# Issue orders in a first stage, and one FFN block wholly in seven-product form

## The chip, the cores and the metric
The kernel runs on one core of a Trainium2 chip. The metric is the device time of one execution in microseconds (us); the median of the runs is compared. Engines: TensorE (PE in the profile, PEld its weight loads), VectorE (DVE), ScalarE (ACT), GpSimd (POOL), and SyncE (SP), whose queue issues the DMAs.

## What is computed
Two pre-norm residual layers on a sequence of 1024 with width 1024, all float32. Layer 0 mixes with a Mamba-2 SSD mixer, layer 1 with a causal Conformer convolution, each is followed by a dense SwiGLU FFN of width 2816, and a final RMSNorm ends it:

```python
for i in range(DEPTH):
    if i % 2 == 0:
        h = h + mamba2_mixer(rmsnorm(h, ssm_norm), w_in, conv_w, ..., w_out)
    else:
        h = h + conformer_conv_module(rmsnorm(h, cv_norm), w_pw1, ..., w_pw2)
    h = h + swiglu_ffn(rmsnorm(h, ffn_norm[i]), ffn_w_gate[i], ffn_w_up[i], ffn_w_down[i])
return rmsnorm(h, final_norm)
```

`mamba2_mixer` projects `u` to 5152 columns (gate, the inputs of a causal convolution of four taps, and 32 columns for `dt`), convolves, runs the state-space scan in chunks of 128, norms with the gate and projects back.

## The kernel before, in words
Activations stand transposed: 128 partitions hold 128 of the 1024 features, the free dimension holds tokens. The sequence is cut into two blocks of 512 tokens (0 and 1), so that one tile is 128x512 and a block of `h` is eight of them. Every matrix product is done three times, on high and low halves of both operands: `split` (L233) makes a high half by a copy on ScalarE and a low half by a subtraction on VectorE (or GpSimd). `gemm` (L255) multiplies low by high, high by low, high by high. Weights come by DMA into `wst` (two buffers), are split into `whi`, `wlo` (four each), and used.

The program is written as a list of units that `run` (L1196) puts together and `emit` (L1285) traces in order; loads are traced ahead of the units that use them. A scheduler then makes each engine's queue: among the instructions that it takes for ready, the one traced first goes first, loads and weight preparation having a head start of 60 places. Queues run strictly in that order on the chip.

**The first stage.** `consts` (L147) makes constants. `begin` (L551) fetches block 0 of `x` and the first three weight tiles of the in-projection, splits them, adds up the squares of `x` and returns the unit `products` (L607), which multiplies three weight tiles and the `dt` columns with the raw `x` times the norm's gain, as the factor that the norm gives each token can be applied to the product. `norm_u` (L324) takes the square sums (`rstd_a`, `rstd_b` with its matmuls at L310), makes the factor, keeps it in `fac`, and writes the normed input `u` in halves, the low ones partly on GpSimd. `in_proj` (L515) makes ten tiles per group of heads: tiles 0 to 3 are made from raw `x` (tile 3 as the unit `r3`), 4 to 9 from `u`. Tiles 0 to 5 go through `conv4` (L492): into a buffer `raws` (by VectorE with `fac`, L503, or by ScalarE, L501), then the four taps; tiles 6 to 9 are the gate. `dt_pre` (L417) transposes the `dt` columns on TensorE (L428) and computes their softplus, `dt_post` (L452) makes decays with small matmuls (L462, L463, L478). `selects` (L185) and `halves` (L209) make small constants. `ssd` (L628) is the scan: `prep`, `A(z)`, `B(z)` (L680, L681), `decay`, `C(z)`. Eight PSUM banks are dealt out by `banks`; a bank is written again only when its reader is done.

**The last FFN.** `ffn` (L925) has two forms. The regular form multiplies each 128 columns of gate and up with `u` in 24 matmuls of 128x512. The fast form, `seven` (L832), treats two column tiles at a time as 2x2 blocks of features and token halves and needs seven block products in place of eight: seven units `p1`, `p2`, `p6`, `p7`, `p5`, `p3`, `p4` of twelve matmuls of 128x256 (L881). For that VectorE sums blocks of the weights (L850 to L852), and `sums_u` (L783) makes sums of blocks of `u` once (tiles `ru`, `tu`). The partial results move out of two shared banks by ScalarE (L892, L901, L908) and VectorE (L897, L909, L917). `chain7` (L1009) orders products of successive tiles and puts down projections (`dn`, L977) between them as soon as their hidden tiles are there. `final` (L1169) norms and sends out a block; its scalings are at L1189.

In the last layer block 0 ends with eight down projections of six tiles. Then block 1 runs two column tiles in the regular form, and twenty in the fast form (groups of 6, 6, 4 and 4). `sums_u(1)` stands between the regular units, `final(0)` after the second and third unit.

Of the kernel before, what the change touches and what calls it, by code (L numbers as in the profile page):

```python
# [43 lines left out]
WARM = 13  # L44
HALO = 30
# [63 lines left out]
class Trunk:  # L109
# [75 lines left out]
    def selects(self):  # L185


        nc = self.nc
        tt = nc.vector.tensor_tensor
        t = self.small.new("sels")  # L190
        rows, one = (t[:, 16 * i:16 * i + 16].rearrange("p (k h) -> p k h", k=2) for i in range(2))
        idg = lambda g: self.ident[:, 32 * g:32 * g + 16].rearrange("p (k h) -> p k h", k=2)
        tt(rows, idg(0), idg(1), ALU.add)
        tt(rows, rows, idg(2), ALU.add)
        tt(rows, rows, idg(3), ALU.add)
        tt(one[:, 0], rows[:, 0], rows[:, 1], ALU.add)
# [9 lines left out]
        nc.vector.tensor_copy(self.sel, one[:, 0].unsqueeze(2).to_broadcast([P, 8, 64]))  # L206
        self.small.drop(t)
# [95 lines left out]
    def rstd_b(self, x, n, tag="ss", w=T):  # L303
# [5 lines left out]
        for k, y in enumerate(x if whole else x[::-1]):  # L309
            nc.tensor.matmul(bc, self.ones if whole else self.onesr, y[:, :w], start=k == 0, stop=k == len(x) - 1)  # L310
# [181 lines left out]
    def conv4(self, b, c, acc, dst, fac=None):  # L492
        nc = self.nc
        raw = self.raws[self.nraw % 2]
        self.nraw += 1
# [19 lines left out]
    def in_proj(self, i, u=None, fac=None):  # L515
# [12 lines left out]
        def run(n):  # L528
# [3 lines left out]
            if n < 2:  # L532
                self.conv4(b, 16 + 4 * n + g, acc, self.c_bc[:, 2 * n + par], fac)
            elif n < 6:
                if n == 2:
                    self.XS[i] = self.big.new("xs")
                self.conv4(b, 4 * g + n - 2, acc, self.XS[i][:, n - 2], fac if n < NR else None)
            else:
                if n == 6:
                    self.SZ[i] = self.big.new("sz")  # L540
                s = self.SZ[i][:, n - 6]
                self.nc.scalar.activation(s, acc, AF.Tanh, scale=0.5)
                self.nc.vector.scalar_tensor_tensor(s, s, 1.0, acc, op0=ALU.add, op1=ALU.mult)
        units = [Unit(lambda n=n: run(n), lambda n=n: load(n)) for n in range(10)]
        if u is not None:
            self.W_in = W
            return [Unit(lambda n=n: gemm(n), lambda n=n: load(n)) for n in range(NB, NR)], [
# [3 lines left out]
    def begin(self, raw, load_dt):  # L551
# [19 lines left out]
        def split_x(d):  # L571
# [3 lines left out]
            nc.vector.scalar_tensor_tensor(lo, x[d], g, hi.bitcast(F32), op0=ALU.mult, op1=ALU.subtract)  # L575
# [9 lines left out]
        fetch_x(0)  # L585
        load_dt()
# [9 lines left out]
        for d in range(KD):  # L596
            split_x(d)
# [28 lines left out]
        return Unit(products), bigs  # L626
# [569 lines left out]
    def run(self):  # L1196
# [6 lines left out]
        self.consts()  # L1203
        self.mixer_setup()
# [3 lines left out]
        r3, ip = self.in_proj(0, raw, fac)  # L1208
# [3 lines left out]
        r3[0].load()  # L1212
        r3[0].load = None
        nu = self.norm_u(0, "ssm_norm", 0, fac, (0, 1, 3, 5, 7))
        q = [products] + nu[:2] + [call(self.halves, fac)] + nu[2:] + r3 + [call(lambda: self.big.drop(*rb))]
        q += dt[1:2] + [call(self.selects)] + dt[2:] + ip[:NR]
        q += [call(lambda: self.small.drop(fac)), call(lambda: self.banks(mm=(0, 1, 2, 3), ss=(4, 5, 6, 7)))] + ip[NR:]
        q += [call(self.load_x, 1)]
        for i in range(8):
# [16 lines left out]
            q += weave(self.ssd(i), fill) + post  # L1236
# [141 lines left out]
```

## Time and profile before

| | us |
|---|---|
| median of 3 runs (lowest, highest) | 2493.28 (2493.01, 2493.83) |
| the profiled execution | 2493.91 |
| its span, first to last instruction | 2492.2 |
| TensorE busy in the span | 2471.1 |
| VectorE busy | 2052.9 |
| ScalarE busy | 1328.7 |
| mean granted TensorE clock | 0.997 |

The profile is of one execution. Times in it are counted from the start of the span. An instruction's row gives start and duration, or the duration of several that follow each other; matmuls are pipelined, so their spacing and not their duration tells what they cost. What a row names as the releaser is what the engine's idle time ended with.

### The profile page before, as it was taken

The page shows a single profiled execution, that of the slowest core. Times are in us where ns is not written, and L with a number is a line of the kernel's source. Part 1 is how long each engine was busy: PE and PEld are TensorE (multiplying, and loading weights), DVE is VectorE, ACT ScalarE, POOL GpSimd, SP SyncE. Part 2 cuts the span into 40 slices and gives each one's busy share as a digit, 9 for nine tenths or more (in the row PEclk, how much of TensorE's full clock was granted, in tenths as well). Part 3 has the DMA queues.
Part 4 walks back from the last instruction along what each step waited for, and adds up shares of the span by engine and source line. Part 5 has one row for each costly group of instructions (what it writes and reads, how often), then busy time and mean ns, then how long its engine had stood idle before and what let it go on. Part 6 is the DMA issues. An engine that isn't in the chain of part 4 may idle for free.

```text
span 2492.2 us, 35811 instructions
## 1 busy us (share of the span) xinstructions
PE 2471.1 (99%) x13752; PEld 2114.9 (85%) x13752; DVE 2052.9 (82%) x3030; ACT 1328.7 (53%) x2365; POOL 398.8 (16%) x406
## 2 busy tenths in 40 slices
PE   8999999999999999999999999999999999999998
PEld 6788887888887899998888789988887899899998
DVE  7988989878889886768799797778997977986675
ACT  5776776766667553545333455453335545554444
POOL 1212111112111000000444410004444100000000
PEclk9999999999999999999999999999999999999999
DMA  4222222222223332323223233232232323332322
GB/s 159 68 68 85 77 62 85 77 73 79 76 70 110 89 112 92 110 67 100 93 93 111 87 114 109 64 102 93 93 119 85 123 91 104 131 118 82 119 85 73
DMA packets 69516, 233.54 MB, mean 94 GB/s; under 512 B 7648, under 2 KB 11232, under 8 KB 61920
## 3 DMA queue, kind: packets, MB, share of 16 engines
q1 hardware_dynamic: 69344, 231.25, 28.5%
q8 instruction: 108, 1.77, 0.3%
q14 instruction: 64, 0.52, 0.1%
HBM read 227.02 MB, written 4.19 MB: 93 GB/s over the span
## 4 chain that ended last, share of the span: by engine, by line
PE 97%; DVE 2%; ACT 1%; issue 0%; DMA 0%; DVEq 0%; SPq 0%; ACTq 0%
PE p L259 68%; PE p L881 23%; PE p L712 1%; PE p L704 1%; PE p L667 1%; PE p L680 1%; PE p L681 1%; PE p L310 0%; PE p L647 0%; PE p L695 0%; DVE wlo L235 0%; PE p L408 0%; PE p L614 0%; PE p L615 0%; PE p L618 0%; DVE un_s L349 0%
## 5 line engine op out<-in xcount | busy, mean ns | idle before, releaser
L234 ACT ACTIVATE whi<-wst 128x512 fp32r<-128x512 f32 (+1 forms) x652 | 388.0, 597 | 689.3 <-PE p L259 577.9
L259 PE MATMUL p<-uhi_b,wlo 128*128 128x512 f32 x1344 | 533.7, 397 | 3.3 <-ACT uhi_b L234 1.8
L259 PE MATMUL p<-ulo_b,whi 128*128 128x512 f32 x1344 | 529.4, 394 | 1.6 <-POOL ulo_b L235 1.1
L259 PE MATMUL p<-uhi_b,whi 128*128 128x512 f32 x1344 | 530.5, 395 | 0.0
L259 PE MATMUL p<-hid_b,whi 128*128 128x512 f32 x1344 | 419.1, 394 | 0.2
L235 DVE TENSOR_TENSOR wlo<-wst,whi 128x512 fp32r<-128x512 f32 (+1 forms) x442 | 303.9, 690 | 123.5 <-ACT whi L234 120.2
L235 POOL TENSOR_TENSOR wlo<-wst,whi 128x512 fp32r<-128x512 f32 x208 | 256.4, 1236 | 724.3 <-ACT whi L234 720.9
L881 PE MATMUL p<-uhi_b,wh_b 128*128 128x256 f32 x1856 | 343.9, 280 | 0.0
L259 PEld LDWEIGHTS p<-uhi_b,wlo 128*128 128x128 f32 x1344 | 253.0, 188 | 62.4 <-ACT uhi_b L234 2.6
L259 PEld LDWEIGHTS p<-ulo_b,whi 128*128 128x128 f32 x1344 | 253.3, 188 | 61.9 <-POOL ulo_b L235 2.9
L259 PEld LDWEIGHTS p<-uhi_b,whi 128*128 128x128 f32 x1344 | 253.1, 188 | 59.2 <-issue 0.3
L259 PEld LDWEIGHTS p<-hid_b,whi 128*128 128x128 f32 x1344 | 251.9, 188 | 56.7 <-DVE hid_b L235 1.1
L881 PEld LDWEIGHTS p<-uhi_b,wh_b 128*128 128x128 f32 x1856 | 290.9, 188 | 3.2 <-ACT vw_s L908 0.8
L259 PE MATMUL p<-hid_b,wlo 128*128 128x512 f32 x672 | 264.3, 394 | 0.0
L881 PE MATMUL p<-ulo_b,wh_b 128*128 128x256 f32 x928 | 259.9, 280 | 0.0
L881 PE MATMUL p<-tu_b,wh_b 128*128 128x256 f32 x1392 | 183.2, 281 | 0.0
L881 PEld LDWEIGHTS p<-ulo_b,wh_b 128*128 128x128 f32 x928 | 174.6, 188 | 2.0
L234 ACT ACTIVATE wh_b<-ws_b 128x1024 fp32r<-128x1024 f32 x116 | 122.7, 1059 | 99.2 <-PE p L881 38.9
L881 PEld LDWEIGHTS p<-tu_b,wh_b 128*128 128x128 f32 x1392 | 173.6, 188 | 1.3
L1097 DVE SCALAR_TENSOR_TENSOR p<-ci_b,par,p 128x507 f32<-128x507 f32 (+29 forms) x240 | 160.3, 733 | 3.3 <-ACT p L1094 2.0
L235 DVE TENSOR_TENSOR wh_b<-ws_b,wh_b 128x1024 fp32r<-128x1024 f32 x116 | 141.1, 1221 | 25.6 <-ACT wh_b L234 25.3
L1099 DVE SCALAR_TENSOR_TENSOR p<-ci_b,par,p 128x512 f32<-128x512 f32 x232 | 158.1, 749 | 1.9 <-ACT p L1094 1.4
(282 smaller groups left out, 4027.1 us busy)
## 6 DMA issues: line engine op xcount, KB each, us to landing
wq_b<-w_gu SPq DMA_DIRECT2D x58, 1024.0 KB, 4.8
wst<-w_in SPq DMA_DIRECT2D x77, 512.0 KB, 3.5
wst<-w_dn SPq DMA_DIRECT2D x88, 384.0 KB, 3.1
wst<-w_gu SPq DMA_DIRECT2D x60, 512.0 KB, 3.5
wst<-w_pw SPq DMA_DIRECT2D x48, 512.0 KB, 3.5
wst<-w_out SPq DMA_DIRECT2D x64, 256.0 KB, 2.6
wst<-w_dn SPq DMA_DIRECT2D x40, 256.0 KB, 2.7
h<-xT SPq DMA_DIRECT2D x8, 512.0 KB, 8.8
```

Source lines behind the costliest of these rows:

```text
L234: self.nc.scalar.activation(hi, src, AF.Copy)
L235: (eng or self.nc.vector).tensor_tensor(lo, src, hi.bitcast(F32), ALU.subtract)
L259: self.nc.tensor.matmul(acc, a, b, start=n == 0, stop=n == tot - 1)
L667: nc.tensor.transpose(xt[:, zs(j)], self.XS[i][:, j, zs(z)], self.ident)
L680: nc.tensor.matmul(sg, self.gtr, aml, start=True, stop=False)
L681: nc.tensor.matmul(sg, self.gtr, amh, start=False, stop=True)
L704: nc.tensor.matmul(O[:, zs(j)], H[:, zs(j)], CT[:, zs(z)], start=True, stop=True)
L712: nc.tensor.matmul(Y[po:po + 64, zs(hh // 2)], self.XDT[z % 2][:, hh * 64:(hh + 1) * 64], E[:, zs(r)], start=True, stop=True)
L881: nc.tensor.matmul(to, x, y, start=n == 0 and not more, stop=n == 11, skip_group_check=True)
L1097: nc.vector.scalar_tensor_tensor(acc[:, s:], x[:, HALO:TW - s], w(s), acc[:, s:], op0=ALU.mult, op1=ALU.add)
L1099: nc.vector.scalar_tensor_tensor(acc if s < 30 else c, x[:, HALO - s:TW - s], w(s), acc, op0=ALU.mult, op1=ALU.add)
```

## The change
In the first stage: `selects` moves to the front and keeps program order on VectorE, and `begin`'s instructions on VectorE go behind it. The squares of `x` keep program order on ScalarE in pairs. `products` is cut in two: tiles 0 to 5 of the features before the norm's matmuls, tiles 6 and 7 and then `r3` behind them. `halves` goes behind the last low half of `x` on VectorE. `conv4` is cut into `conv4a` (into the buffer) and `conv4b` (the taps); the unit `evict` does `conv4a` for tiles 0 to 3 at once, into the two `raws` and two spare stretches of `ms`. `dt_post` goes on TensorE behind the last matmul of tile 7, with the priority of the place ahead of tile 0's unit; the first three units of `ssd(0)` go on TensorE behind the last matmul of tile 9. Seven banks are dealt to `mm` and one to `ss` until tile 5. `issue_after(ins)` orders only instructions of the engine of `ins`, and only their issue.

In the last FFN: all 22 column tiles of block 1 take the fast form (groups of 6, 6, 6 and 4); `sums_u(1)` and the norm of block 1 move in between the last down projections of block 0.

```diff
+NP = 6
     def selects(self):
-        nc = self.nc
-        tt = nc.vector.tensor_tensor
+        nc, keep = self.nc, self.tc.keep_in_program_order
+        tt = lambda *a: keep(nc.vector.tensor_tensor(*a))
...
-    def conv4(self, b, c, acc, dst, fac=None):
-        nc = self.nc
-        raw = self.raws[self.nraw % 2]
-        self.nraw += 1
+        self.conv4b(b, c, self.conv4a(b, c, acc, fac), dst)
+
+    def conv4a(self, b, c, acc, fac=None, raw=None):
+        nc = self.nc
+        if raw is None:
+            raw = self.raws[self.nraw % 2]
+            self.nraw += 1
...
+        def evict():
+            ms = self.c_ms.rearrange("p a t -> p (a t)")
+            spare = [ms[:, 1014 + 516 * k:1014 + 516 * k + T + 3] for k in range(2)]
+            for n, raw in enumerate(self.raws + spare):
+                W["raw", n] = True
+                W["acc", n] = self.conv4a(b, 16 + 4 * n + g if n < 2 else 4 * g + n - 2, W["acc", n], fac, raw)
...
+        def square(d):
+            to = s if d == 0 else self.small.new("sq")
+            self.tc.keep_in_program_order(nc.scalar.activation(to, x[d], AF.Square))
+            if d:
+                nc.vector.tensor_tensor(s, s, to, ALU.add)
+                self.small.drop(to)
...
-            if d > 1:
-                self.sq_add(("h", 0), x[d - 2])
-        for d in range(KD - 2, KD):
-            self.sq_add(("h", 0), x[d])
+            if d % 2:
+                square(d - 1)
+                square(d)
...
+        def rest(r3):
+            with self.tc.issue_after(self.norm_mm.ins):
+                products(NP, KD)
+                r3()
+        return lambda r3: [Unit(lambda: products(0, NP)), Unit(lambda: rest(r3))], bigs
...
         self.consts()
+        self.selects()
...
-        self.banks(mm=(0, 1, 2, 3, 4, 5), ss=(6, 7))
+        self.banks(mm=(0, 1, 2, 3, 4, 5, 7), ss=(6,))
         self.warm(WARM)
-        products, rb = self.begin(raw, dt[0].load)
+        with self.tc.issue_after(self.last_sel.ins):
+            products, rb = self.begin(raw, dt[0].load)
...
-        q = [products] + nu[:2] + [call(self.halves, fac)] + nu[2:] + r3 + [call(lambda: self.big.drop(*rb))]
-        q += dt[1:2] + [call(self.selects)] + dt[2:] + ip[:NR]
-        q += [call(lambda: self.small.drop(fac)), call(lambda: self.banks(mm=(0, 1, 2, 3), ss=(4, 5, 6, 7)))] + ip[NR:]
+        def behind(run, prio=None):
+            def f():
+                keep = self.tc.cur_priority
+                if prio:
+                    self.tc.cur_priority = prio[0]
+                with self.tc.issue_after(self.mm.ins):
+                    run()
+                if prio:
+                    self.tc.cur_priority = keep
+            return Unit(f)
+        def halves():
+            with self.tc.issue_after(self.last_lo.ins):
+                self.halves(fac)
+        def here():
+            self.mm = self.last_mm
+        q = products[:1] + nu[:2] + products[1:] + [call(halves)] + nu[2:] + [evict]
+        q += [call(lambda: self.big.drop(*rb))] + dt[1:2] + [call(lambda: self.small.drop(fac)), call(mark)] + ip[:6]
+        q += [call(lambda: self.banks(mm=(0, 1, 2, 3), ss=(4, 5, 6, 7)))] + ip[6:8]
+        q += [call(here), behind(dt[2].run, at_dt)] + ip[8:] + [call(here)]
...
+            steps = self.ssd(i)
+            if i == 0:
+                steps[:3] = [behind(u.run) for u in steps[:3]]
+            q += weave(steps, fill) + post
...
-        q += [call(self.phase7)] + put(c, *at(n1, (-10, -8, -7, -6, -5)))
+        su = self.sums_u(1)
+        q += [call(self.phase7)] + put(c, *at(n1, (-10, -9, -8, -7, -6)), *at(su, (-4, -3, -2)))
         f0, f1, f2 = self.final(0), self.final(1, (0,)), self.final(1, (HT,))
-        c = self.chain7(self.ffn(1, 0, 2, [1]), fast(1, 2, 6, [1]), fast(1, 8, 6, [1]), fast(1, 14, 4, [1]),
+        c = self.chain7(fast(1, 0, 6, [1]), fast(1, 6, 6, [1]), fast(1, 12, 6, [1]),
                         fast(1, 18, 4, [1], [1], True), free=1, hold=4)
-        q += put(c, *at(self.sums_u(1), (1, 2, 4)), (2, f0[:1]), (3, f0[1:]), *at(f1, (-7, -5, -4, -3, -2))) + f2
+        q += put(c, (2, f0[:1]), (3, f0[1:]), *at(f1, (-7, -5, -4, -3, -2))) + f2
```

## Rows read from the trace of the kernel before
**Rows 1.** The page: busy us of each engine; the chain by engine.
```profile
PE 2471.1 (99%) x13752; PEld 2114.9 (85%) x13752; DVE 2052.9 (82%) x3030; ACT 1328.7 (53%) x2365; POOL 398.8 (16%) x406
...
PE 97%; DVE 2%; ACT 1%; issue 0%; DMA 0%; DVEq 0%; SPq 0%; ACTq 0%
```
**Rows 2.** TensorE's waits, 29 to 84 us, last from 84 on: sum, times, longest.
```profile
PE p L680 <- ACT am_b L663: 3.1, 1, 3.1
PE p L259 <- DVE sf_b L503: 1.5, 1, 1.5
PE p L259 <- ACT uhi_b L234: 1.3, 1, 1.3
PE p L259 <- POOL ulo_b L235: 1.1, 2, 0.9
...
PE p L680 <- DVE sz_b L726: 0.6, 1, 0.6
```
**Rows 3.** Timeline of TensorE, 29 to 87 us: start, us, instruction, count [idle before].
```profile
29.05 0.39 PE L310 MATMUL p<-suml_s,onesr 128*128 128x512 f32 x1
...
34.77 0.40 PE L259 MATMUL p<-rhi_b,whi 128*128 128x512 f32 x1
...
37.83 0.51 PE L259 MATMUL p<-ulo_b,whi 128*128 128x512 f32 x1 [0.87 <-POOL ulo_b L235]
...
45.35 1.04 PE L428 MATMUL p<-sf_b,dtraw_s 64*128 64x32 f32 x8 [0.78 <-DVE sels_s L193]
...
86.09 0.83 PE L647 MATMUL p<-bct_b 128*128 128x128 f32 x6
```
**Rows 4.** The chain in order of time: start, us, what; both matmul sizes.
```profile
29.67 5.51 PE p L259 x24
...
2073.86 26.89 PE p L881 x228
```
**Rows 5.** Stretches: us, busy PE, PEld, DVE, ACT, POOL (count), clock, DMA.
```profile
65.00:70.00 5.00, 3.44 (x7) 2.32 (x8) 4.96 (x9) 3.97 (x9) 1.83 (x3) 0.50 0.00 0
...
23.20:86.10 62.90, 54.34 (x221) 41.23 (x220) 51.32 (x96) 34.25 (x66) 14.85 (x24) 0.92 0.21 73
86.10:160.00 73.90, 73.87 (x397) 60.76 (x396) 63.35 (x94) 51.03 (x111) 15.99 (x22) 1.00 0.23 73
```
**Rows 6.** Timeline of VectorE, 20 to 40 us.
```profile
22.48 0.69 DVE L235 TENSOR_TENSOR suml_s<-ssum_s,sumh_s 128x512 fp32r<-128x512 f32 x1
...
37.85 1.71 DVE L235 TENSOR_TENSOR ulo_b<-un_s,uhi_b 128x512 fp32r<-128x512 f32 x1
```
**Rows 7.** Timeline of TensorE, first products.
```profile
9.13 0.50 PE L614 MATMUL p<-rhi_b,am_b 128*128 128x512 f32 x1 [0.45 <-DVE am_b L235]
```
**Rows 8.** Timeline of VectorE: two 512-wide splits in a row.
```profile
13.61 1.29 DVE L235 TENSOR_TENSOR er_x<-H_b,er_x 128x512 fp32r<-128x512 f32 x2
```
**Rows 9.** Stretches in the last FFN, columns as in rows 5.
```profile
2101.90:2137.70 35.80, 35.80 (x165) 29.23 (x165) 33.59 (x54) 20.01 (x37) 0.00 (x0) 1.00 0.47 155
2137.70:2149.00 11.30, 11.30 (x50) 9.18 (x50) 10.96 (x15) 9.10 (x13) 0.00 (x0) 1.00 0.19 58
```
**Rows 10.** Timeline of VectorE, 2103 to 2170 us.
```profile
2103.32 0.69 DVE L315 SCALAR_TENSOR_TENSOR p<-p,rstd_s 128x512 f32<-128x512 f32 x1
...
2142.16 2.36 DVE L235 TENSOR_TENSOR tu_b<-ru_b,tu_b 128x1024 fp32r<-128x1024 f32 x2
...
2162.33 5.35 DVE L1189 SCALAR_TENSOR_TENSOR h<-h,par,p 128x512 f32<-128x512 f32 x8
...
2168.80 0.41 DVE L897 TENSOR_TENSOR hx_x<-vw_s,p 128x256 f32<-128x256 f32 x1
```
**Rows 11.** The chain in order of time: down projections of block 0 and behind.
```profile
2104.31 50.02 PE p L259 x215
```
**Rows 12.** Timeline of TensorE, 2169 to 2172 us.
```profile
2170.36 0.52 PE L881 MATMUL p<-tu_b,wh_b 128*128 128x256 f32 x3
2170.72 1.10 PE L259 MATMUL p<-hid_b,whi 128*128 128x512 f32 x4
```

More of the change, by code (lines that the diff above doesn't have):

```diff
@@ L205, in selects @@
         tt(self.mine.unsqueeze(2), m[:, :, 0:1], m[:, :, 1:2], ALU.add)
-        nc.vector.tensor_copy(self.sel, one[:, 0].unsqueeze(2).to_broadcast([P, 8, 64]))
+        self.last_sel = keep(nc.vector.tensor_copy(self.sel, one[:, 0].unsqueeze(2).to_broadcast([P, 8, 64])))
         self.small.drop(t)
@@ L258, in gemm @@
             for a, b in ((wl, xh), (wh, xl), (wh, xh)):
-                self.nc.tensor.matmul(acc, a, b, start=n == 0, stop=n == tot - 1)
+                self.last_mm = self.nc.tensor.matmul(acc, a, b, start=n == 0, stop=n == tot - 1)
                 n += 1
@@ L309, in rstd_b @@
         for k, y in enumerate(x if whole else x[::-1]):
-            nc.tensor.matmul(bc, self.ones if whole else self.onesr, y[:, :w], start=k == 0, stop=k == len(x) - 1)
+            self.norm_mm = nc.tensor.matmul(bc, self.ones if whole else self.onesr, y[:, :w], start=k == 0,
+                                            stop=k == len(x) - 1)
         self.small.drop(*x)
@@ L505, in conv4, with conv4b @@
             nc.gpsimd.tensor_copy(self.carry[:, c], raw[:, T:])
+        return raw
+    def conv4b(self, b, c, raw, dst):
+        nc = self.nc
         v = self.small.new("v")
@@ L531, in run @@
             acc = W.pop(("acc", n))
[L532 to L537, printed above, removed]
+            c = 16 + 4 * n + g if n < 2 else 4 * g + n - 2
+            if n == 2:
+                self.XS[i] = self.big.new("xs")
+            if n < 6:
+                raw = acc if ("raw", n) in W else self.conv4a(b, c, acc)
+                self.conv4b(b, c, raw, self.c_bc[:, 2 * n + par] if n < 2 else self.XS[i][:, n - 2])
             else:
@@ L546, in in_proj @@
             self.W_in = W
-            return [Unit(lambda n=n: gemm(n), lambda n=n: load(n)) for n in range(NB, NR)], [
+            return Unit(lambda: gemm(NB), lambda: load(NB)), Unit(evict), [
                 Unit(lambda n=n: run(n)) for n in range(NR)] + units[NR:]
@@ L574, in split_x @@
             nc.scalar.activation(hi, x[d], AF.Copy, scale=g)
-            nc.vector.scalar_tensor_tensor(lo, x[d], g, hi.bitcast(F32), op0=ALU.mult, op1=ALU.subtract)
+            self.last_lo = nc.vector.scalar_tensor_tensor(lo, x[d], g, hi.bitcast(F32), op0=ALU.mult, op1=ALU.subtract)
+        def square(d):
[4 more added lines that the diff above has]
+                self.small.drop(to)
+        s = self.sums["h", 0] = self.small.new("ssum")
         def split_w(n, k):
@@ L585, in begin @@
         fetch_x(0)
+        split_x(0)
         load_dt()
@@ L596, in begin, with products @@
         for d in range(KD):
-            split_x(d)
+            if d:
+                split_x(d)
             for n, k in weights.get(d, ()):
                 split_w(n, k)
-            if d > 1:
-                self.sq_add(("h", 0), x[d - 2])
-        for d in range(KD - 2, KD):
-            self.sq_add(("h", 0), x[d])
+            if d % 2:
+                square(d - 1)
+                square(d)
         step, W_in = self.dt_step, self.W_in
         W = [[(cut(to[n][0], k), cut(to[n][1], k)) for k in range(KD)] for n in range(NB)]
-        def products():
-            acc = [self.bank("mm") for _ in range(NB)]
-            for k in range(KD):
+        acc = []
+        def products(k0, k1):
+            if k0 == 0:
+                acc.extend(self.bank("mm") for _ in range(NB))
+            for k in range(k0, k1):
                 xh, xl = raw[k]
@@ L620, in products @@
                 W_in["acc", n] = acc[n]
+            if k0:
+                return
             keep = self.bank("ss")
@@ L1207, in run @@
         dt = self.dt_path(0, raw, fac)
-        r3, ip = self.in_proj(0, raw, fac)
-        self.banks(mm=(0, 1, 2, 3, 4, 5), ss=(6, 7))
+        r3, evict, ip = self.in_proj(0, raw, fac)
+        self.banks(mm=(0, 1, 2, 3, 4, 5, 7), ss=(6,))
         self.warm(WARM)
-        products, rb = self.begin(raw, dt[0].load)
-        r3[0].load()
-        r3[0].load = None
+        with self.tc.issue_after(self.last_sel.ins):
+            products, rb = self.begin(raw, dt[0].load)
+        r3.load()
+        products = products(r3.run)
         nu = self.norm_u(0, "ssm_norm", 0, fac, (0, 1, 3, 5, 7))
-        q = [products] + nu[:2] + [call(self.halves, fac)] + nu[2:] + r3 + [call(lambda: self.big.drop(*rb))]
-        q += dt[1:2] + [call(self.selects)] + dt[2:] + ip[:NR]
-        q += [call(lambda: self.small.drop(fac)), call(lambda: self.banks(mm=(0, 1, 2, 3), ss=(4, 5, 6, 7)))] + ip[NR:]
+        at_dt, mark = [], lambda: at_dt.append(self.tc.cur_priority)
+        def behind(run, prio=None):
[17 more added lines that the diff above has]
+        q += [call(here), behind(dt[2].run, at_dt)] + ip[8:] + [call(here)]
         q += [call(self.load_x, 1)]
```

2 lines of the change are left out of this document (removed).

## Prediction
> **What bounds the kernel now.** I read the page's busy times and chain first: TensorE is busy for 99% of the span and carries 97% of the chain [rows 1], so only its waits, its slow stretches and its own work can move the end. TensorE's waits come next. Between 29 and 84 us seven of them add up to 8.4 us, 3.1 us the longest; from 84 to 2453 us the longest is 0.6 us [rows 2]. So what can be won by order lies in the first stage.
>
> There the timeline gives the whole loss, stalled slots and slow clock included. The last matmul on raw `x` starts at 34.77, so its slot ends at 35.0; at 86.09 `prep` starts, with all six tiles 4 to 9 of the first in-projection done [rows 3]. In these 51.1 us stand 144 matmuls of 128x512, which run 24 in 5.51 us (0.2296 each) [rows 4], 33.1 us; the small matmuls between them (transposes 1.0, `dt_post` 0.9, `B(0)` 0.5, two of `prep` 0.2) make 2.6. That leaves 15.4 us lost: the 8.4 of waits, slots partly missed around them, and half clock: the stretch 65 to 70 us was granted 0.50, which is 1.2 GHz, after TensorE had stood 3.1 us [rows 2, 5].
>
> **Part 1, the first stage.** (a) `products` is cut after the sixth of eight tiles. The squares' sum is ready at 23.2 (its low half is written from 22.48 for 0.69) [rows 6], while TensorE reaches the norm's two matmuls only at 29.05 [rows 3]. With 22 products (two tiles, 11 each) and the 24 of tile 3 put behind them, the norm starts at about 24 and 46 x 0.2296 = 10.6 us of matmuls cover it. The cover needed is 29.05 to 37.83 = 8.8 us to the first low half of `u` [rows 3]. So the first two waits (1.3 and 1.1 us) go. The next seven low halves came over about 7.2 us (37.83 to 45.0), and TensorE wants one every 0.69: 8.8 + 7.2 - 10.6 - 4.8 = 0.6 us stay lost.
>
> (b) The first four accumulators are multiplied by `fac` and put into SBUF together (`evict`: four 0.6 us multiplies on VectorE, behind the norm), so no later bank waits for VectorE: the 1.5 us wait goes. `dt_pre` is behind them and its eight transposes are still placed freely in TensorE's queue, as at 45.35 where TensorE stood for them [rows 3]; the norm and the transposes now share bank 6. I keep 1.0 us lost, between 0 and 2.
>
> (c) `dt_post`, `prep`, `A(0)` and `B(0)` issue on TensorE only behind tiles 7 and 9. Their VectorE and ScalarE chains then have some 20 to 30 us of tiles in front of them: the 3.1 us wait and the slow clock behind it go. Queued behind a late one is the second in-projection, which is ready; its loads are not held.
>
> (d) What is late next is VectorE. From 23.2 to 86.1 it is busy 51.3 of 62.9 us, from 86.1 to 160 for 63.4 of 73.9 [rows 5]: 22.1 us idle in 136.8, and TensorE would reach the same point 15 us sooner. The twenty small operations of `selects`, about 0.1 us each, leave this stretch (now before 5.8, when VectorE waits for `x`: free), so 112.7 us of work in 121.5, 93%. That fits, barely; in the last FFN it holds 94% without a TensorE wait [rows 9]. I take 1.5 us lost, bounds 0 and 6. (e) The squares move behind the first weight splits; TensorE waited 0.45 us for one at 9.13, with two squares ahead of it on ScalarE [rows 7]; the load may have landed only then: gain 0 to 0.45, taken 0.2. `halves` moved behind the last low half of `x`: 0.5 us of VectorE, hidden in a stretch with 6 us idle.
> Sum of part 1: -15.4 + 0.6 + 1.0 + 1.5 - 0.2 = **-12.5**, bounds -15.6 and -7.
>
> A row on (a): VectorE's split of `u` at 37.85 took 1.71 us while GpSimd split others; the same form takes 0.69 elsewhere [rows 6, 8]. The Trainium skill, page "SBUF — State Buffer", section "SBUF: two separate sides", says that GpSimd and a VectorE operation with two SBUF inputs exclude each other for a whole instruction. By it the three VectorE halves here would each lose a full GpSimd operation; by the row they lose 1 us or less, and the sum has that in its 7.2 us.
>
> **Part 2, TensorE's work.** 96 matmuls of 128x512 go: 96 x 0.2296 = 22.0 us. Two more seven-product tiles come: 168 matmuls of 128x256, which run 228 in 26.89 us (0.118) [rows 4]: 19.8. The down projections regroup (2+6+6+4+4 tiles to 6+6+6+4) with the same matmuls. **-2.2 us**.
>
> **Part 3, what VectorE pays for that.** The regular tiles cost VectorE little; seven products cost it 1024-wide sums and splits. In the stretch before and around them VectorE is already full: 33.6 of 35.8 us, then 11.0 of 11.3 [rows 9]. I make a running sum. Pitches: 0.60 us for a 512-wide operation (two in 1.29), 0.66 for a scaled one (eight in 5.35), 1.14 for a 1024-wide one (two in 2.36), half of 0.66 for 256 wide [rows 8, 10]. The down projections of block 0 start at 2104.31 (0.2327 us apart [rows 11]), 144 of them end at T = 2137.8; then block 1 starts. VectorE can begin the norm of block 1 at 2101.9 (2103.32 less one product, 1.4, since its unit moves one place up).
>
> Before the sixth product of the second pair can start, 15 products after T (T + 21.2 = 2159.0), VectorE must have done: the norm, 3 steps of 0.72, 8 scalings, 8 splits, 12.2; the rest of block 0's last pair (768, 1024 and two 256 wide), 2.7; of eight down projections 6 wide and 7 half-wide splits, 8 adds to `h`, 8 for the square sum, 15.5; `sums_u`, 8 of 1.14, 9.1; the weights of gate and up, each 4 of 1024 and 3 of 512, 12.7; of the next gate 2 of 1024 for sums and a split, 2 of 512, one more split, 4.6; six evictions of 256, 2.0; block 0's `final`, 3 steps and 8 scalings, 7.4, which the list puts after three products. Together 66.2 us. From 2101.9 there are 57.1: **9.1 us short**, 1.7 if `final` yields to the rest.
>
> The same sum on the kernel before, up to 2170.4, gives 69.6 needed (regular tiles 7.2 and two-tile down projections 3.5 among it) of 67.1: 2.5 short, and there the trace shows it. The eviction on which the seventh product waits ran at 2168.80, behind the eight scalings of `final` [rows 10], and TensorE alternates single products with matmuls of down projections [rows 12]. Those filled the gap. In the changed kernel the first down projection of block 1 is due 49 products, 69 us, after T, so nothing fills. Since products with ready inputs can still go out of turn, I take 7.5 us of waits, bounds 1.7 and 13 (9.1 plus what 94% use adds on 66 us). The output transfers of `final` stand in SP's queue ahead of weight loads and wait for VectorE too; that is in the upper bound.
>
> The wait of 3.1 us was followed by 5 us at 1.2 GHz with 7 matmuls in them [rows 5], 7 x 0.23 = 1.6 us lost. Waits of 2 to 3 us here may or may not do that: 0 to 2, taken 0.5. The Trainium skill, "TensorE: Matmul & The Clock Gate", section "What's actually happening", has the slow clock as the default that activity lifts and idleness brings back; by it these waits would cost the 1.6, and the sum would be 1.1 us higher.
> Part 2 and 3: -2.2 + 7.5 + 0.5 = **+5.8**, bounds -0.5 and +12.8.
>
> **Sum.** -12.5 + 5.8 = -6.7. The profiled execution took 2493.91 (span 2492.2, 1.7 outside it), 0.6 above the median of the runs: 2493.28 - 6.7 = **2486.6**.
>
> **Rivals.** (1) VectorE keeps up in the last FFN: `final` and the late squares yield, the wait is 1.7 or nothing. For it: TensorE shows no wait there now. Against: the sum above. -12.5 - 2.2 + 0.5 = -14.2: 2479.1. (2) The first stage gives back half: the work ahead of TensorE runs out once tiles 4 to 9 are through, since VectorE has only 9 us to spare until 160. -7 + 5.8 = -1.2: 2492. (3) Slower: in block 1's first pairs `final`'s scalings hold evictions, the evictions hold banks and the load queue; it decides once these waits with their slow clock pass 14 us while the first stage gives its 7 only (7 + 2.2 + the 5 that can be told); at 18 it is -7 - 2.2 + 18 = +8.8: 2502. Against: 13 is the most that the sum bears. (4) The orders bind only within one engine's queue, so VectorE and ScalarE may still run in the old order and the 3.1 us wait moves to tile 9's end; that is (2) in time.
>
> **How the numbers follow.** Forecast 0.55, (1) 0.22, (2) with (4) 0.18, (3) 0.05. The range goes from just below rival 1 to rival 2 plus 2: 2478 to 2494. A measurement tells 0.2%, 5 us, from no change: faster is below 2488.3. Of the forecast about two thirds lie there (0.36), all of (1), little of (2): faster 0.60; same 0.34; slower 0.06.
>
> **What would show it.** Right: the norm's matmuls near 24 us; no TensorE wait above 1 us from 30 to 100; the six tiles done near 72; granted clock 1.00 throughout; then, some 5 to 30 us after block 1's first seven products begin, TensorE waits on VectorE (evictions L897, splits, `tu`), with `final`'s scalings ahead of them and VectorE above 95%. Wrong: no such waits (rival 1), or new waits on VectorE between 70 and 160 us (rival 2).

## The result, and the profile after

The changed kernel is slower: 2499.73 us (11 runs, 2497.51 to 2502.18) beside 2493.83 for the kernel before (11 runs, 2492.54 to 2494.30), a ratio of 1.0024 with a 95% interval of 1.0016 to 1.0032. The forecast, 2486.6 in 2478 to 2494, is wrong by 13 us. The first stage saved 5.6 us, less than its worst bound of 7, and the last FFN cost 12.1, near its upper bound of 12.8. All times below are of the profiled executions, and the place in the program is named with them.

| | before | after | difference |
|---|---|---|---|
| profiled execution, us | 2493.91 | 2500.46 | +6.6 |
| its span | 2492.2 | 2498.7 | +6.5 |
| TensorE busy | 2471.1 | 2469.1 | -2.0 |
| VectorE busy | 2052.9 | 2057.5 | +4.6 |
| end of the last product on raw `x` | 35.0 | 37.5 | +2.5 |
| `prep`, all six tiles done | 86.1 | 80.2 | -5.9 |
| first product of block 1 in the last FFN | 2137.8 | 2132.2 | -5.6 |
| from there to the end of the span | 354.4 | 366.5 | +12.1 |

The page of after first, busy times and chain, which answer [rows 1]. TensorE's share of the chain fell from 97% to 93%, and VectorE's rose from 2% to 5%.

```profile
PE 2469.1 (99%) x13824; PEld 2117.7 (85%) x13824; DVE 2057.5 (82%) x3033; ACT 1335.1 (53%) x2370; POOL 402.5 (16%) x406
...
PE 93%; DVE 5%; ACT 1%; DMA 1%; issue 0%; SPq 0%; DVEq 0%; ACTq 0%
```

TensorE's waits in after, over the whole span (sum, times, longest). The waits of [rows 2] on `am_b`, `sf_b` and `ulo_b` are gone, and others stand in their place; all of 0.9 us and more are on VectorE.

```profile
PE p L916 <- DVE wh_b L236: 7.9, 4, 3.0
PE p L260 <- DVE wlo L236: 4.0, 2, 2.9
PE p L642 <- DVE er_x L236: 1.9, 1, 1.9
...
PE p L916 <- DVE hx_x L932: 1.0, 1, 1.0
PE p L260 <- DVE wdn_b L236: 0.9, 1, 0.9
```

The timeline of TensorE says where they lie (lines are those of the changed kernel: L642, L643, L646 are the products on raw `x`, L260 `gemm`, L682 `prep`, L916 the seven products).

```profile
10.00 0.50 PE L642 MATMUL p<-rhi_b,xd_b 128*128 128x512 f32 x1 [0.78 <-DVE xd_b L236]
13.82 0.50 PE L642 MATMUL p<-rhi_b,er_x 128*128 128x512 f32 x1 [1.94 <-DVE er_x L236]
26.47 0.39 PE L311 MATMUL p<-suml_s,onesr 128*128 128x512 f32 x1
37.29 0.39 PE L260 MATMUL p<-rhi_b,whi 128*128 128x512 f32 x1
57.48 0.51 PE L260 MATMUL p<-uhi_b,wlo 128*128 128x512 f32 x1 [1.09 <-DVE wlo L236]
73.03 0.50 PE L260 MATMUL p<-uhi_b,wlo 128*128 128x512 f32 x1 [2.89 <-DVE wlo L236]
80.24 1.06 PE L682 MATMUL p<-bct_b 128*128 128x128 f32 x8
...
2136.92 1.62 PE L916 MATMUL p<-tu_b,wh_b 128*128 128x256 f32 x12 [1.59 <-DVE wh_b L236]
2141.53 0.36 PE L916 MATMUL p<-uhi_b,wh_b 128*128 128x256 f32 x1 [2.99 <-DVE wh_b L236]
2145.51 0.58 PE L916 MATMUL p<-uhi_b,wh_b 128*128 128x256 f32 x1 [2.12 <-DVE wh_b L236]
2166.57 0.36 PE L916 MATMUL p<-uhi_b,wh_b 128*128 128x256 f32 x1 [1.22 <-DVE wh_b L236]
2170.62 1.69 PE L916 MATMUL p<-tu_b,wh_b 128*128 128x256 f32 x12 [0.98 <-DVE hx_x L932]
2474.53 1.69 PE L260 MATMUL p<-hid_b,wdn_b 128*128 128x256 f32 x12 [0.89 <-DVE wdn_b L236]
```

In the last FFN 228 products of 128x256 and two of the norm's matmuls stand between 2132.22 and 2172.14. At the spacing of [rows 4] they take 228 x 0.118 + 0.5 = 27.4 us, and they took 39.9: **12.5 us lost**. 8.9 are the five waits. The rest is half clock behind them and slots partly missed around them. The windows (columns as in rows 5) show it at both places, and the chain in order of time shows what it costs: 24 matmuls in 7.38 where 5.51 is usual, 48 in 7.77 where 5.7 is.

```profile
70.00:75.00 5.00, 2.11 (x8) 1.66 (x8) 5.00 (x9) 4.59 (x9) 0.10 (x1) 0.93 0.07 14
75.00:80.00 5.00, 5.00 (x17) 3.90 (x17) 2.27 (x4) 0.63 (x1) 0.00 (x0) 0.73 0.54 196
...
2142.00:2147.00 5.00, 2.88 (x18) 2.59 (x17) 5.00 (x8) 2.60 (x3) 0.00 (x0) 0.58 0.00 0
2147.00:2152.00 5.00, 5.00 (x34) 5.00 (x34) 5.00 (x6) 3.12 (x6) 0.00 (x0) 0.74 0.11 16
```

```profile
73.03 7.38 PE p L260 x24
...
2145.51 7.77 PE p L916 x48
```

VectorE's timeline there: the weight halves `wh_b` on which TensorE waits come behind the sums and their splits (`tu_b` in the rows) and behind additions that end block 0, with no idle row from 2104 to 2155. `final`'s eight scalings come only later; one weight half and one eviction stand behind them.

```profile
2132.68 1.22 DVE L236 TENSOR_TENSOR tu_b<-ru_b,tu_b 128x1024 fp32r<-128x1024 f32 x1
...
2135.55 1.22 DVE L236 TENSOR_TENSOR wh_b<-ws_b,wh_b 128x1024 fp32r<-128x1024 f32 x1
...
2140.16 1.22 DVE L236 TENSOR_TENSOR wh_b<-ws_b,wh_b 128x1024 fp32r<-128x1024 f32 x1
...
2144.24 1.22 DVE L236 TENSOR_TENSOR wh_b<-wq_b,wh_b 128x1024 fp32r<-128x1024 f32 x1
...
2159.94 5.35 DVE L1224 SCALAR_TENSOR_TENSOR h<-h,par,p 128x512 f32<-128x512 f32 x8
2165.21 1.22 DVE L236 TENSOR_TENSOR wh_b<-ws_b,wh_b 128x1024 fp32r<-128x1024 f32 x1
```

### The profile page after: what moved, and what is told of

It is laid out like the page before. It is cut to its first block, busy times and chain, and to the rows that moved or that the text cites. A ratio compares the mean times of both kernels' runs of the same rounds, so it can differ in the third digit from the quotient of the medians.

```text
span 2498.7 us, 35927 instructions
## 1 busy us (share of the span) xinstructions
PE 2469.1 (99%) x13824; PEld 2117.7 (85%) x13824; DVE 2057.5 (82%) x3033; ACT 1335.1 (53%) x2370; POOL 402.5 (16%) x406
## 4 chain that ended last, share of the span: by engine, by line
PE 93%; DVE 5%; ACT 1%; DMA 1%; issue 0%; SPq 0%; DVEq 0%; ACTq 0%
PE p L260 64%; PE p L916 23%; PE p L747 1%; PE p L739 1%; DVE wlo L236 1%; PE p L702 1%; DVE v_s L520 1%; PE p L715 1%; PE p L716 1%; DMA wst<-w_dn 0%; PE p L311 0%; DVE ulo_b L236 0%; DVE un_s L351 0%; PE p L682 0%; PE p L730 0%
## 5 line engine op out<-in xcount | busy, mean ns | idle before, releaser
L260 PE MATMUL p<-uhi_b,wlo 128*128 128x512 f32 x1312 | 520.3, 397 | 4.5 <-DVE wlo L236 4.0
L260 PE MATMUL p<-uhi_b,whi 128*128 128x512 f32 x1312 | 517.5, 394 | 0.0
L260 PE MATMUL p<-ulo_b,whi 128*128 128x512 f32 x1312 | 516.0, 393 | 0.1
L260 PE MATMUL p<-hid_b,whi 128*128 128x512 f32 x1344 | 419.4, 393 | 0.2
L916 PE MATMUL p<-uhi_b,wh_b 128*128 128x256 f32 x1920 | 357.5, 281 | 6.3 <-DVE wh_b L236 6.3
L916 PEld LDWEIGHTS p<-uhi_b,wh_b 128*128 128x128 f32 x1920 | 302.2, 189 | 10.1 <-issue 3.2
L260 PEld LDWEIGHTS p<-hid_b,whi 128*128 128x128 f32 x1344 | 251.9, 188 | 57.3 <-DVE hid_b L236 1.1
L260 PEld LDWEIGHTS p<-uhi_b,wlo 128*128 128x128 f32 x1312 | 246.6, 188 | 61.8 <-DVE wlo L236 5.3
L260 PEld LDWEIGHTS p<-uhi_b,whi 128*128 128x128 f32 x1312 | 246.7, 188 | 57.7 <-issue 0.3
L260 PEld LDWEIGHTS p<-ulo_b,whi 128*128 128x128 f32 x1312 | 246.8, 188 | 57.6 <-issue 0.7
L916 PE MATMUL p<-ulo_b,wh_b 128*128 128x256 f32 x960 | 269.8, 281 | 0.0
L260 PE MATMUL p<-hid_b,wlo 128*128 128x512 f32 x672 | 264.4, 394 | 0.0
L916 PE MATMUL p<-tu_b,wh_b 128*128 128x256 f32 x1440 | 189.8, 281 | 2.6 <-DVE wh_b L236 1.6
L916 PEld LDWEIGHTS p<-tu_b,wh_b 128*128 128x128 f32 x1440 | 179.7, 189 | 4.1 <-ACT sq_s L273 1.8
L916 PEld LDWEIGHTS p<-ulo_b,wh_b 128*128 128x128 f32 x960 | 181.6, 189 | 1.7
L236 DVE TENSOR_TENSOR wh_b<-ws_b,wh_b 128x1024 fp32r<-128x1024 f32 x120 | 146.1, 1221 | 27.6 <-ACT wh_b L235 27.4
```

Source lines behind the costliest of these rows:

```text
L236: (eng or self.nc.vector).tensor_tensor(lo, src, hi.bitcast(F32), ALU.subtract)
L260: self.last_mm = self.nc.tensor.matmul(acc, a, b, start=n == 0, stop=n == tot - 1)
L916: nc.tensor.matmul(to, x, y, start=n == 0 and not more, stop=n == 11, skip_group_check=True)
```

## The experiments

### The two parts alone

**a1_stage1** is the changed kernel with the last FFN of the kernel before, **a2_lastffn** the kernel before with the changed last FFN.

> The change's first stage alone, the last FFN as before. Theory (the two parts add up): in the changed kernel's trace the last FFN's block 1 starts at 2132.2 in place of 2137.8, so this part is worth -5.6 us: 2488.2 beside 2493.8. Rival (the two parts hang together, the time won at the front is lost again at the end whatever stands there): within 1 us of the kernel before. The prediction's own term for this part was -12.5: 2481.3.

> The change's last FFN alone, the first stage as before. Theory (the parts add up): from block 1's start to the end the changed kernel took 366.5 us, the kernel before 354.4, so +12.1: 2505.9. Rival (the waits come of where the front part left the loads): +6 or less, 2500. The prediction's own term was +5.8: 2499.6.

Measured, beside 2493.61: a1 2488.76 (0.9981, interval 0.9972 to 0.9990), a2 2505.37 (1.0047, 1.0034 to 1.0059). They are -4.9 and +11.8, together +6.9 where the whole change gave +5.9. The parts add up within 1 us; both rivals fall.

### The first stage

**a4_start_undone** takes a1 and gives up the new order at the very start:

```diff
-        self.selects()                       (ahead of mixer_setup)
-        with self.tc.issue_after(self.last_sel.ins):
-            products, rb = self.begin(raw, dt[0].load)
+        products, rb = self.begin(raw, dt[0].load)
-            if d % 2:
-                square(d - 1)
-                square(d)
+            if d > 1:
+                self.sq_add(("h", 0), x[d - 2])
...
-        q += ... + dt[1:2] + [...]
+        q += ... + dt[1:2] + [call(self.selects), ...]
```

> The first stage's part without its new order at the very start: selects back behind dt_pre, the square sums and begin's instructions free as before; the cut of products, evict and the orders behind tiles 7 and 9 stay; last FFN as before. Theory (the start's order costs 2.5 us, since the last matmul on raw x ended at 37.5 in place of 35.0): 2.5 below the run with the whole first stage, 2485.7. Rival (what the start gives up VectorE has back later, as selects' small operations stand in the backlog at 45 to 75 us again): no better than the whole first stage, 2488 to 2489.

Measured 2487.56 (0.9976, 0.9967 to 0.9986). The last product on raw `x` starts at 34.51 (34.77 before, 36.87 in a1), so the start's order does cost 2.4 us there. By the medians only 1.2 of it arrive at the end: in place of a1's two waits of 1.0 and 2.9 us TensorE now has one of 5.0. Each expectation held half. TensorE's timeline, and under it VectorE's and ScalarE's, show that wait:

```profile
65.44 0.80 PE L260 MATMUL p<-uhi_b,wlo 128*128 128x512 f32 x1 [4.97 <-DVE wlo L236]
```

```profile
56.76 0.75 DVE L520 SCALAR_TENSOR_TENSOR v_s<-sf_b,v_s 128x512 f32<-128x512 f32 x1
57.42 0.78 DVE L520 SCALAR_TENSOR_TENSOR v_s<-ms_b,sf_b,v_s 128x512 f32<-128x512 f32 x1
58.13 0.37 DVE L462 TENSOR_TENSOR sr_b<-sf_b,sr_b 128x128 fp32r<-128x128 f32 x1
58.42 3.63 DVE L520 SCALAR_TENSOR_TENSOR v_s<-ms_b,sf_b,v_s 128x512 f32<-128x512 f32 x3
...
64.05 0.74 DVE L520 SCALAR_TENSOR_TENSOR v_s<-ms_b,sf_b,v_s 128x512 f32<-128x512 f32 x1
64.71 0.68 DVE L236 TENSOR_TENSOR wlo<-wst,whi 128x512 fp32r<-128x512 f32 x1
```

```profile
51.39 0.63 ACT L235 ACTIVATE whi<-wst 128x512 fp32r<-128x512 f32 x1 [0.21 <-DMA wst<-w_in]
...
59.29 0.61 ACT L235 ACTIVATE whi<-wst 128x512 fp32r<-128x512 f32 x1
```

Counted in order, the low half made at 64.71 is VectorE's eleventh 512-wide one of these weights, and ScalarE's eleventh high half is done at 52.0; the last that it makes before the wait ends is done at 59.9. So neither ScalarE nor a load holds it. VectorE starts the low half 12.7 us after that high half, behind taps of tiles 0 to 3 that nobody waits for yet. Three kernels ask whether VectorE's work is the cause and whether its amount or its order is. **b3_taps** leaves work out, **b4_weng** moves the low halves away, **c1_gates_first** keeps the work and turns the order:

```diff
+        for k in (2, 1) if b == 0 and c in (0, 1, 2, 3, 16, 20) else (2, 1, 0):     (b3, conv4b)
...
+            if i == 0 and n > 4:                                                    (b4, in_proj's load)
+                self.weng = self.nc.gpsimd
...
-        ... ip[:6] + [banks] + ip[6:8] + [here, dt_post] + ip[8:]
+        ... ip[6:8] + ip[:2] + ip[4:6] + ip[2:4] + [banks] + [here, dt_post] + ip[8:]       (c1)
```

> The run with the start undone, and the last tap of the convolution left out in the six tiles of block 0's first group (part of the computation is left out): six VectorE operations of 0.66 us, 4.0 us, go from 45 to 75 us. Theory (VectorE's backlog holds the weights' low half for which TensorE stands 5.0 us at 65): the wait falls to about 1 us and the slow clock behind it goes: 2487.6 - 5.5 = 2482. Rival (a late load or ScalarE's high half holds it): no change, 2487.

> The run with the start undone, and the low halves of the weights of tiles 5 to 9 of the first in-projection on GpSimd in place of VectorE: 10 splits. Theory (they stand in VectorE's queue behind taps that nobody waits for): 6 us off VectorE and out of its queue, the 5.0 us wait and its slow clock go: 2480.5. Rival (GpSimd's splits, 1.24 us alone and 1.7 beside VectorE, are late themselves or slow VectorE's taps): a wait of 2 us or more stays, 2485 or above.

> The run with the start undone, and the order of the first group's units turned: the two gate tiles 6 and 7 first, whose reader is one VectorE operation, then the taps of 0 and 1, tiles 4 and 5, the taps of 2 and 3, tiles 8 and 9. The same work; taps stand behind the next tiles' weight halves. Theory (what counts is the work that stands ahead of a due step in VectorE's queue, not the sum over the stage): the 5.0 us wait falls below 1.5 and the slow clock goes: 2487.6 - 5 = 2482.5. Rival (the sum over the stage is too much, the wait only moves to prep): 2486 or above.

Measured: b3 2481.95 (0.9953, 0.9941 to 0.9966), b4 2486.17 (0.9970, 0.9958 to 0.9981), c1 2483.80 (0.9960, 0.9948 to 0.9973). Four us of VectorE less give 5.6 us: VectorE's backlog is the cause. The same work in another order gives 3.8 of them, so most of the loss is what stands ahead in the queue; c1's longest wait here is 1.5 us, on a tile of the scan's input. GpSimd helps little (b4, 1.4 us): TensorE's longest wait becomes 1.8 us on VectorE's part of `dt_post`, with 0.8 to 0.9 on GpSimd.

**c4_not_behind** takes a4 and drops the holds behind tiles 7 and 9 on TensorE together with `dt_post`'s early priority; **d2_no_prio** drops the priority alone and keeps the holds.

```diff
-        q += [call(here), behind(dt[2].run, at_dt)] + ip[8:]
+        q += [call(here), Unit(dt[2].run)] + ip[8:]                  (c4)
+        q += [call(here), behind(dt[2].run)] + ip[8:]                (d2)
...
-                steps[:3] = [behind(u.run) for u in steps[:3]]       (c4 alone)
```

> The run with the start undone, and dt_post and the scan's first three units no longer held behind tiles 7 and 9 on TensorE. The prediction's step (c): these orders take away a wait of 3.1 us and its slow clock; without them it comes back beside the 5.0 us wait: 2487.6 + 4 = 2491.5. Rival (the cut of products and evict already carry the gain, VectorE's backlog sets the time with or without these orders): 2487 to 2488.

> The run with the start undone, with dt_post traced behind tile 7 with the priority of that place and not of the place ahead of tile 0; it and the scan's first units stay held behind tiles 7 and 9 on TensorE. If dt_post's early place in VectorE's queue costs the 4.4 us that the run without both gained: 2483 to 2484. If the holds cost it (prep can't fill TensorE's wait): 2487 to 2488.

Measured: c4 2483.16 (0.9958, 0.9944 to 0.9971), d2 2483.64 (0.9959, 0.9944 to 0.9973), where a4 had 2487.56. Both expectations on c4 missed: the orders were neither needed nor neutral. The 3.1 us wait on `am_b` did not come back, and it is `dt_post`'s place, not the holds, that costs 4 us. TensorE's longest wait from 20 to 110 us is 2.4 us in d2 and 1.2 in c4, where a4 had 5.0. VectorE's timeline of d2 shows how:

```profile
56.58 0.68 DVE L236 TENSOR_TENSOR wlo<-wst,whi 128x512 fp32r<-128x512 f32 x1
57.18 4.06 DVE L520 SCALAR_TENSOR_TENSOR v_s<-ms_b,sf_b,v_s 128x512 f32<-128x512 f32 x6
```

A weight half (by count the one that a4 makes at 64.71) goes ahead of the taps, and six taps take 4.06 us, 0.67 each. In a4 `dt_post` was due early, its small operations took that place, and GpSimd's two operations for the scan (`am_b`, 2.49 us from 58.36) ran beside three taps, which took 3.63 in place of 2.0. c4 is the fastest kernel that computes everything: 0.4% faster than the kernel before.

### The last FFN

**b1_final_late** puts `final(0)` behind product 40, **c2_late** puts it behind 44 and block 0's square sum behind products 24 to 38, both in the changed kernel.

```diff
-        q += put(c, (2, f0[:1]), (3, f0[1:]), ...
+        q += put(c, (40, f0[:1]), (41, f0[1:]), ...                                               (b1)
+        q += put(c, *at(self.x_sums(0), range(24, 40, 2)), (44, f0[:1]), (45, f0[1:]), ...        (c2)
```

> The changed kernel with final(0) behind product 40 of block 1 in place of 2 and 3. Theory (VectorE has too much due before the first two pairs, whatever final does): the waits on weight halves at 2135 to 2146, 1.6 + 3.0 + 2.1 us with their slow clock, stay; only the two behind the eight scalings, 1.2 and 1.0 us, go: 2499.7 - 2.2 = 2497.5. Rival (final's scalings hold back what TensorE needs): all these waits go, 8.9 us and the slow clock: 2488.

> The changed kernel with final(0) behind product 44 of block 1 and block 0's square sum, eight squares on ScalarE and seven additions on VectorE, put behind products 24 to 38 in place of between the down projections. The same work, later. Theory (VectorE has too much due before block 1's first two pairs): beside the run with final late alone, 2495.3, 7 x 0.60 = 4.2 us leave that stretch, so its waits of 6.7 us fall to about 2.5 and their slow clock mostly goes: 2489.5. Rival (the additions go where VectorE waits anyway): no better than 2494.

Measured: b1 2495.33 (1.0008, 0.9999 to 1.0017), c2 2493.09 (0.9997, 0.9988 to 1.0006). In b1's trace (of its longest execution, 2498.51) the waits of 1.2 and 1.0 us behind the scalings are gone and the three before them stand as they were:

```profile
PE p L916 <- DVE wh_b L236: 6.7, 3, 3.0
```

So `final` is about a third of the loss, 4.4 us by the medians, 2.2 of it waits. Seven additions put later give 2.2 us more, where the theory for c2 had 5.8. In c2's trace 2.9 and 0.5 us are left of those 6.7; the execution in it is one of c2's two fastest (2489.90).

**b2_gpsimd** gives the low halves of block 1's `u` and block 0's square additions to GpSimd:

```diff
-        n1 = self.norm_u(1, "ffn_norm", 8, whole=True)
+        n1 = self.norm_u(1, "ffn_norm", 8, None, range(KD), True)
...
+                self.sq_add(("h", b) + part, h, add=nc.gpsimd if l and not part else None, ...)
```

> The changed kernel with VectorE relieved where block 0 ends: the eight low halves of block 1's normed input and the seven additions of block 0's last square sum run on GpSimd, which does nothing there. Theory (VectorE's time is what is short): 15 operations at 0.60 are 9 us, so the waits of 6.7 us at 2135 to 2146 and their slow clock go: 2490. Rival (the order of the queue, not the amount, or GpSimd's halves at 1.24 us come too late for the sums): 2497 or more.

Measured 2503.80 (1.0043, 1.0030 to 1.0057), 4.1 us slower than the changed kernel. GpSimd's halves were not late for the sums, which start at 2113.91 where the changed kernel has 2121.93. One GpSimd and one VectorE line of its timeline, and the same VectorE operation later, with GpSimd idle:

```profile
2121.28 1.49 POOL L284 TENSOR_TENSOR ssum_s<-ssum_s,sq_s 128x512 f32<-128x512 f32 x1 [2.29 <-ACT sq_s L273]
```

```profile
2121.53 1.78 DVE L886 TENSOR_TENSOR ws_b<-wq_b,ws_b 128x512 f32<-128x512 f32 x1
...
2143.27 0.68 DVE L886 TENSOR_TENSOR ws_b<-wq_b,ws_b 128x512 f32<-128x512 f32 x1
```

VectorE's operation took 1.1 us more while GpSimd's ran. Twelve of its lines between 2103 and 2148 are longer than their usual form, by 10.0 us in all; the 15 operations taken from it were worth 9.0. That leaves VectorE no gain. TensorE's longest wait is 4.8 us there, for a weight half made at 2159.94, right behind `final`'s eight scalings; how the 4.1 us divide was not tested.

**a3_moved** and **c3_moved_two** keep the two regular tiles and move only the norm and the sums, a3 all three units of the sums, c3 the first two. In a3 the third unit overwrites a part of `u` that the regular tiles then multiply, so its values are others and the tiles wait for it.

```diff
-        q += [...] + put(c, *at(n1, (-10, -8, -7, -6, -5)))
+        q += [...] + put(c, *at(n1, (-10, -9, -8, -7, -6)), *at(su[:2], (-4, -3)))       (c3)
-        q += put(c, *at(self.sums_u(1), (1, 2, 4)), ...
+        q += put(c, *at(su[2:], (4,)), ...
```

> Of the last FFN's change only the move: the norm of block 1 one place up and its sums between the last down projections of block 0; block 1 keeps its two regular tiles. Theory (VectorE's work in all is what is short, and the two regular tiles give it 11 us): no wait above 1 us on TensorE, 2493.8, within 1.5. Rival (the moved sums stand ahead of weight splits and this order alone makes the waits): 3 to 7 us of waits, 2497 to 2501.

> The kernel before with the norm of block 1 one place up and the first two units of its sums between the last down projections of block 0; the third, which overwrites a part of u, stays behind the regular tiles. Theory (the seven-product form makes the shortage, since two regular tiles ask VectorE for little in 11 us): 2493.8, within 1.5. Rival (the moved sums themselves push weight halves and additions back): TensorE waits 2 us or more at the end of block 0, 2496 to 2499.

Measured: a3 2501.04 (1.0030, 1.0019 to 1.0042), c3 2500.15 (1.0026, 1.0016 to 1.0036). The theory, that only the seven-product form makes the shortage, falls: with regular tiles the move alone costs 6.4 us. In c3 the sums' splits stand ahead of the additions that free the banks:

```profile
2140.57 1.22 DVE L235 TENSOR_TENSOR tu_b<-ru_b,tu_b 128x1024 fp32r<-128x1024 f32 x1
2141.72 1.88 DVE L985 TENSOR_TENSOR h<-h,p 128x512 f32<-128x512 f32 x3
```

```profile
2142.45 0.80 PE L259 MATMUL p<-uhi_b,wlo 128*128 128x512 f32 x1 [3.85 <-DVE h L985]
```

**d1_sums_late** asks whether the place of the sums is then the whole cause: the changed kernel with only them put back. **d3_all_late** has c4's first stage and all of it late.

```diff
-        q += [...] + put(c, *at(n1, (...)), *at(su, (-4, -3, -2)))
+        q += [...] + put(c, *at(n1, (...)))
-        q += put(c, (2, f0[:1]), ...
+        q += put(c, *at(su, (0, 0, 0)), (2, f0[:1]), ...
```

> The changed kernel with only the three units of block 1's sums put back behind the last down projection of block 0, ahead of block 1's first product. The same work. Theory of order (the sums stand ahead of additions and weight halves that TensorE needs first): a gain of 3 us or more, 2496 or below. Theory of amount (the first three products need all of it anyway): the waits only change their place, 2499.7 within 1.5.

> The first stage of the run without the start's order and without the holds (2483.2), and the changed last FFN with all that can wait put later: block 1's sums behind block 0's last down projection, block 0's square sum behind products 24 to 38, final(0) behind product 44. Theory of amount: block 1's first pairs still ask for more than VectorE has, some 3 us of waits and slow clock stay, 2483.2 - 2.2 + 3 to 5 = 2484 to 2486. Theory of order: nothing is lost, and the two seven-product tiles give their 2.2 us: 2481.

Measured: d1 2503.60 (1.0039, 1.0024 to 1.0054), d3 2488.29 (0.9978, 0.9968 to 0.9987). The sums late are 3.9 us worse; TensorE then waits 4.9 us for their first split, and the later products for the next ones. On d1 both theories missed. d3 is 5.1 us slower than c4, 2.3 more than the most that amount foretold. Its waits at the first products:

```profile
2135.20 0.39 PE L908 MATMUL p<-tu_b,wh_b 128*128 128x256 f32 x1 [2.01 <-ACT tu_b L235]
2137.52 2.71 PE L908 MATMUL p<-tu_b,wh_b 128*128 128x256 f32 x11 [1.93 <-DVE tu_b L236]
```

So in the last FFN both hold: early, the sums push back what ends block 0; late, block 1's third product waits for them. There was no place among those tried where they cost nothing: beside kernels with the same first stage and the old last FFN, early sums with the rest late cost 4.3 us (c2 beside a1), late sums 5.1 (d3 beside c4). The reason that fits the rows is that VectorE has no idle time up to block 1 while the seven-product form asks for the sums three products in; no run left work out of this stretch to test it, as b3 did in the first stage.

## Why the prediction was wrong

**What bounds the kernel** held: only waits, slow stretches and TensorE's own work moved the end.

**Part 1, -12.5 foretold, -5.6 measured.** (a) and (b) held: the norm's matmuls moved up to 26.47, which is 24.0 without the start's 2.5 (23.68 in a4), the waits for `u` are 0.5 us and the `dt_pre` transposes cost 0.5 in place of 1.0. (c) was wrong in what it credited: the 3.1 us wait is away without the orders too (c4), and the early place of `dt_post` that comes with them costs 4 us (d2). (d) is the term that failed: 1.5 us with bounds 0 to 6. After has 1.1 and 2.9 us of waits on weight halves, and the half clock behind the second costs 7.38 - 5.51 = 1.9, 5.9 us together. The wait that ends at 73.03 is the sign that the prediction had named for rival 2. The sum of VectorE's work over 137 us said that it fits; b3 and c1 show that the work ahead of each weight half in VectorE's queue decides, and that half is due tens of us earlier than the end of the stretch. Those runs stand on a4; the changed kernel's rows of ScalarE and VectorE show the same at 73 us, a low half (by count) 10 us behind its high half:

```profile
61.70 0.62 ACT L235 ACTIVATE whi<-wst 128x512 fp32r<-128x512 f32 x1
```

```profile
72.30 1.28 DVE L236 TENSOR_TENSOR wlo<-wst,whi 128x512 fp32r<-128x512 f32 x2
```

(e) was taken as a gain of 0.2 and is a loss of 2.5 at its place: TensorE's queue now has tile 2's first product (`er_x`) right behind the first two features', and stands 1.9 us for its weight half, which VectorE makes at 13.08; before, products of the third feature with `am_b` and `xd_b` stood ahead of it, from 12.31 to 14.87. a4 undoes the whole of that start; which piece of it does this, no run tells. One reading was wrong by a count: the 8.4 us [rows 2] were eight waits, not seven.

**Part 2, -2.2.** TensorE's busy time, half clock included, fell by 2.0.

**Part 3, +7.5 of waits and 0.5 of clock foretold; 12.1 + 2.2 = 14.3 lost.** The sum of VectorE's work found 9.1 us short, and the five waits are 8.9, but that agreement is partly luck. The sum looked at one due point, 15 products in. Three of the waits, 6.7 us, end 4.7, 9.3 and 13.3 us into block 1, ahead of it; and with `final` out of the way the sum leaves 1.7 us, where TensorE in b1 still waited 6.7. So this step failed as (d) did: it summed to one end point and not to each moment at which a result is due. The value taken, 7.5, allowed for products going out of turn; at each of the five waits TensorE stood. The term that was mis-sized is the clock, 0.5: 12.5 - 8.9 = 3.6 us of half clock and partly missed slots in block 1's first pairs, where the bound was 2. The Trainium skill, page "TensorE: Matmul & The Clock Gate", section "What's actually happening", has idleness bring the slow clock back; after's windows agree at both places, with 0.73 and 0.58, while behind c2's single wait of 2.9 us the clock stayed at 1.00. The end of the kernel adds 1.5, from the first matmul on `wdn_b` to the end 35.1 us in place of 33.6, with a wait of 0.9 on the last down projections' weights; that was not foreseen, and no run settles its cause. Named rightly were the engine and the stretch. The waits end 4.7, 9.3, 13.3, 34.4 and 38.4 us after block 1's start, so the 5 to 30 us hold for three of them at most, and `final`'s scalings stood ahead of the last two only.

**The rivals.** The first stage gave back half, as rival 2 said, and the last FFN cost near the upper bound at the same time. The range ended at 2494 because these were priced as separate cases, though both are waits for VectorE's queue where TensorE gets ahead of it. Rival 3 had the side and nearly the time, but its mechanism, scalings that hold evictions, is 2.2 of the 8.9 us (b1).

**The row weighed in (a).** The prediction allowed 1 us or less where VectorE and GpSimd work side by side [rows 6]. b2 shows 1.1 for one operation, and how it adds up to 10.0: VectorE's 0.68 became 1.78 while one GpSimd operation of 1.49 ran. The Trainium skill, page "SBUF — State Buffer", section "SBUF: two separate sides", has the two exclude each other for a whole instruction; by it VectorE waits out what is left of GpSimd's operation, and here the trace agrees, with 1.1 us lost where 1.24 of GpSimd's were left.

## What to carry to other kernels

Before moving work forward on an engine as full as VectorE was here (93% by the prediction's sum), list what then stands ahead of each result that TensorE waits for, at the first moment at which it is due; a sum over the whole stretch says only whether it fits at the end. An order that takes one wait away is worth testing alone, as its early work may be what makes the next wait. Price waits of 2 to 3 us with the half clock that can follow them: here 1.9 us behind one of 2.9.

## What the hardware showed

GpSimd took little or nothing off a full VectorE where both work on SBUF: 15 operations moved, worth 9.0 us, made others 10.0 us longer (b2), ten splits moved gave 1.4 us (b4), and three taps beside GpSimd took 3.63 in place of 2.0 (a4). In b2's same stretch VectorE's additions with one input in PSUM (L1020) kept their 0.67.

Half clock behind a wait is not the same in every execution. The changed kernel spreads over 4.7 us, from 2497.5 at a mean clock of 0.998 to 2502.2 at 0.996, and c2 over 4.8, from 2489.9 at 0.999 to 2494.7 at 0.996; c4, whose longest wait behind the start is 1.2 us, stays within 0.2 over 4 runs at 0.999. A long wait alone does not spread them: the kernel before, with one of 3.1 us, stays within 1.8 over 11 runs, a4, with one of 5.0, within 1.7 over 9. In the profiled execution of c2 the 2.9 us wait was followed by a granted clock of 1.00, in that of after the stretches with and behind the waits of 3.0 and 2.1 us had 0.58 and 0.74; what decides it stays open.
